# First projections of a hybrid decoder layer: modulation sums queued behind weight low parts, h made two k-tiles at a time, one pace constant changed

## The chip, the cores and the metric

The kernel runs on 1 core of one Trainium2 chip. The metric is the device time of one execution in microseconds (us). Before the change the median of 3 runs is 1785.43 us, from 1785.31 to 1785.56 us.

## The reference, cut to what matters

One decoder layer, 256 tokens of width 2048, float32. The parts that the change touches are the first lines of the reference:

```python
mod = (jax.nn.silu(c) @ w_ada[l] + b_ada[l]).reshape(B, N_MOD, 1, D)
sh1, sc1, gt1, sh2, sc2, gt2 = (mod[:, j] for j in range(N_MOD))
h = rmsnorm(x, g_mix[l]) * (1.0 + sc1) + sh1
z = h @ w_in[l]
```

`silu(c) @ w_ada` is a vector times a 2048 x 12288 matrix. Its first two parts, the shift `sh1` and the scale `sc1`, are needed before `h` exists, and `h` is needed before any product with `w_in` (2048 x 16392). From `z` come three token mixers (an mLSTM, a differential attention and a stick-breaking attention); then follow a projection of each branch, a gated sum, an output projection and a gated MLP. None of these later parts is touched.

## The kernel before, in words

**Precision by splitting.** TensorE multiplies in a rounded float format (fp32r). Each float32 operand is therefore split: ScalarE (ACT) rounds a copy, the high part `hi`; VectorE (DVE) subtracts, the low part `lo = raw - hi`. A product is three matmuls (hi x hi, hi x lo, lo x hi). For weights this is `weights()` (L338 to L355): a DMA of up to four k-tiles (4 x 128 rows by 512 or 440 columns) into a raw tile, then for every two k-tiles one ACT cast (L349) and one DVE subtraction (L351). `state["split"]` always holds the low-part instruction written last.

**The modulation on DVE.** `sh1` and `sc1` aren't computed on TensorE. DVE does multiply-adds over the rows of `w_ada`: `acc += raw[k-tile] * c[k-tile]` with one value of c per partition (`ada_mac`, L225 to L232). TensorE then adds up the 128 partitions with small matmuls against ones (`ada_sums`, L243), DVE adds the bias and the gain (L254 to L256), and `make_h` follows. `ada_first` covers two k-tiles of h at a time (k-tiles 0, 1 and then 2, 3); `ada_quad` covers four (4 to 7, 8 to 11, 12 to 15), with 16 multiply-adds of 128x1024 each. A quad's raw tiles hold two of its 16 rows-of-tiles, 1 MB, loaded by two DMAs of 512 KB (L287).

**make_h** (L465): for every k-tile, ACT applies scale and shift to the normalised, transposed x into a temporary `ht` (L476, from the pool `small`, which has 3 buffers of 256 columns), ACT casts it into the high half of `h1` (L425), and DVE subtracts the low half (L426). k-tiles 0 and 1 go another way (L472 to L474), which the change leaves as it is.

**Rounds.** As h comes in pieces, the 13 column groups of the first projections are worked on in rounds over the k-tiles there are (`visit`, L568, and `partial`, L528): groups 0 to 8 over k-tiles 0 and 1; groups 9 to 12 over 0 to 3; groups 0 to 8 over 2 and 3; groups 0 to 9 over 4 to 7; groups 10 to 12 over 4 to 11; groups 0 to 6 over 8 to 11; then all to the end. Between rounds the partial sums lie in SBUF. Groups 0 to 5 are stick-breaking's queries, keys and values, groups 6 to 12 the two gates of the mLSTM and differential attention's inputs in pieces of 440 columns.

**Pace.** After each column group `tick()` runs (L209). It adds `rates["ada"]` to a counter and lets the modulation's generator make as many steps as the counter holds in whole numbers; a step of `ada_quad` is one multiply-add (and, every second time, the two DMA issues before it). The last argument of `visit` is that rate.

**Order.** The framework's scheduler lays down each engine's instructions at build time. It replays the program with its own estimate of the times; an instruction may go ahead of others on its engine that were written before it, if by that replay it is ready sooner. On the chip every engine then runs its list in that order. `tc.issue_after(x)` forbids the instructions written under it to go ahead of `x` on the same engine. In the kernel before it is used for loads (L286: a modulation load goes behind the last weight load on SyncE, the DMA queue called SP) and for the late modulation's multiply-adds (L302), and not for those of `ada_quad` (L290).

**Buffers.** Weight loads of four k-tiles and modulation loads share four raw tiles of 1 MB (`raw_tile`, L217: three of pool `rawp` and slot `s3`), so a load on SP waits until an earlier raw tile has been read to the end, by an L351 or by an L232, and every load behind it on SP waits too. Weights of two k-tiles (groups 0 to 8 over k-tiles 0, 1 and 2, 3) use another pool (L340).

**`sidewide`** (L73) is a pool of 4 buffers of 512 columns; before the change `make_h` doesn't use it. `late_vectors` (L138) holds two of them while it turns small parameter vectors.

Of the kernel before, what the change touches and what calls it, by code (L numbers as in the profile page):

```python
# [12 lines left out]
AF = mybir.ActivationFunctionType  # L13
# [5 lines left out]
S = 256  # L19
# [20 lines left out]
def kernel(  # L40
# [29 lines left out]
    def wide(name):  # L70
        return tmp.tile([P, 512], F32, tag="wide", name=name, bufs=3)

    def sidewide(name):  # L73
        return tmp.tile([P, 512], F32, tag="sidewide", name=name, bufs=4)

    def small(name):
        return tmp.tile([P, 256], F32, tag="small", name=name, bufs=3)

    V, A, T = nc.vector, nc.scalar, nc.tensor
# [113 lines left out]
    state = {"ada": 0.0, "side": 0.0, "split": None, "load": None, "hold": None, "h": 0, "spare": None}  # L193
# [23 lines left out]
    def raw_tile(nk, n, name):  # L217

        if state["spare"] is not None:
            state["spare"] += 1  # L220
            if state["spare"] % 4 == 0:
                return slots.tile([P, nk, n], F32, tag="s3", name=name)
        return rawp.tile([P, nk, n], F32, tag="raw", name=name)

    def ada_mac(accs, raw, kt0, nk):  # L225
        for k in range(nk):
            kt = kt0 + k
            acc = accs[kt % len(accs)]
            if kt < len(accs):
                V.tensor_scalar(acc, raw[:, k, :], ccol[:, kt:kt + 1], None, ALU.mult)  # L230
            else:
                state["mac"] = V.scalar_tensor_tensor(acc, raw[:, k, :], ccol[:, kt:kt + 1], acc, ALU.mult, ALU.add)  # L232
# [10 lines left out]
    def ada_sums(accs, k0, nk):  # L243

        pm = adaps.tile([P, 512], F32, tag="adaps", name="pm")
        for i, acc in enumerate(accs):
            for k in range(2 * nk):
                m = T.matmul(pm[:, k:k + 1], lhsT=acc[:, k * P:(k + 1) * P], rhs=ones[:, 0:1],  # L248
                             start=k + i == 0, stop=i == len(accs) - 1, skip_group_check=True)
        if k0 == 0:  # L250
            with tc.issue_after(m.ins):
                spin(4)
        ks = slice(k0, k0 + nk)
        V.tensor_tensor(b1[:, ks], pm[:, 0:nk], bsh1_c[:, ks], ALU.add)  # L254
        V.tensor_tensor(a1[:, ks], pm[:, nk:2 * nk], bsc1_c[:, ks], ALU.add)
        V.tensor_tensor(a1[:, ks], a1[:, ks], gmix_c[:, ks], ALU.mult)  # L256
        make_h(k0, k0 + nk)
# [22 lines left out]
    def ada_quad(k0, acc):  # L280

        for q in range(8):
            raw = raw_tile(2, 1024, "raw4")
            for i in range(2):
                r0, c0 = q * 256, i * D + k0 * P
                with tc.issue_after(state["load"].ins):  # L286
                    nc.sync.dma_start(raw[:, :, i * 512:(i + 1) * 512],  # L287
                                      w_ada[r0:r0 + 256, c0:c0 + 512].rearrange("(k p) f -> p k f", p=P))
            for k in range(2):
                ada_mac([acc], raw[:, k:k + 1, :], 2 * q + k, 1)  # L290
                yield
        ada_sums([acc], k0, 4)

# [38 lines left out]
    a1 = const.tile([P, KD], F32, name="a1")  # L332
    b1 = const.tile([P, KD], F32, name="b1")
# [89 lines left out]
    def split(hi, lo, src):  # L423

        A.copy(hi, src)  # L425
        return V.tensor_tensor(lo, src, hi.bitcast(F32), ALU.subtract)  # L426


    h1 = [slots.tile([P, KD // 2, 2 * S], F32R, tag=t, name="h1") for t in ("hh", "hl")]
# [3 lines left out]
    xnT_k = lambda kt: xnT[kt // 8][:, (kt % 8) * S:(kt % 8 + 1) * S]  # L433
# [29 lines left out]
            A.copy(xnT[k2 // 4][:, (k2 % 4) * 512:(k2 % 4 + 1) * 512], pb)  # L463

    def make_h(kt0, kt1):  # L465
        ts = []
        for kt in range(kt0, kt1):
            t = small("ht")
            ts.append(t)
            hi, lo = hact[0](kt), hact[1](kt)  # L470
            if kt0 == 0:
                A.activation(hi, xnT_k(kt), AF.Identity, scale=a1[:, kt:kt + 1], bias=b1[:, kt:kt + 1])  # L472
                V.tensor_scalar(t, xnT_k(kt), a1[:, kt:kt + 1], b1[:, kt:kt + 1], ALU.mult, ALU.add)
                state["split"] = V.tensor_tensor(lo, t, hi.bitcast(F32), ALU.subtract)  # L474
            else:
                A.activation(t, xnT_k(kt), AF.Identity, scale=a1[:, kt:kt + 1], bias=b1[:, kt:kt + 1])  # L476
                state["split"] = split(hi, lo, t)
        if kt0 == 0:
            state["first"] = state["split"]
        state["h"] = kt1  # L480
# [47 lines left out]
    def partial(ci, kt0, kt1):  # L528
        orient, col0, n, dest, scale = first[ci]
        while state["h"] < kt1:  # L530
            pump(ada, 1)
        if kt0 == 0 and ci == 0:
            state["first"], done = state["mac0"], state["first"]
        pin = kt0 == 0 and ci < 2
        if kt0 == 0 and ci < 2:
            kept[ci] = [bank("kept"), bank("kept")]
        acc = kept.get(ci)


        put = acc is None and 0 < kt0 and kt1 < KD and not (kt1 == 4 and ci in (6, 8))  # L540
        if put:
            acc = [gp.tile([P, 512], F32, tag="gp", name="gp") for _ in range(2)]
            for b in range(2):
                for cs, d in dest(b):
                    A.copy(shaped(acc[b][:, cs], d), d)
        acc = gemm(orient, hact, w_in, 0, col0, n, kt0, kt1, hold=state["first"] if pin else None, hold_all=pin,
                   acc=acc)
        if kt0 == 0 and ci == 0:
            state["first"] = done
        for b in range(2):  # L550
            for cs, d in dest(b):
                if ci in kept:
                    if kt1 == KD:
                        A.activation(d, shaped(acc[b][:, cs], d), AF.Copy, scale=scale)
                elif put or kt0 == 0:
                    A.copy(d, shaped(acc[b][:, cs], d))
                else:
                    V.scalar_tensor_tensor(d, shaped(acc[b][:, cs], d), scale, d, ALU.mult, ALU.add)
        tick()
# [3 lines left out]
    quads = slot(4, "quads")  # L563
    ada.append(ada_first(2))
    ada.extend(ada_quad(k0, quads[:, (i % 2) * 1024:(i % 2 + 1) * 1024]) for i, k0 in enumerate((4, 8, 12)))
    done = [0] * 13

    def visit(cis, kt1, rate):  # L568
        rates["ada"] = rate
        for ci in cis:  # L570
            partial(ci, done[ci], kt1)
            done[ci] = kt1

    visit(range(0, 9), 2, 0.62)
    visit(range(9, 13), 4, 1.9)
    visit(range(0, 9), 4, 1.0)
    side.append(late_vectors())
    rates["side"] = 0.4
    visit(range(0, 10), 8, 1.72)
# [343 lines left out]
    for ch in range(2):  # L923
        acc = gemm("T", hact, w_in, 0, C_MO + ch * 512, 512, 0, KD)
# [6 lines left out]
    for ch in range(2):  # L931
        acc = gemm("T", hact, w_in, 0, C_MV + ch * 512, 512, 0, KD)
# [5 lines left out]
    for t, col0, f0 in ((mqT, C_MQ, 0), (mkT, C_MK, 8)):  # L938
        for ch in range(2):
            acc = gemm("H", h1act, w_in, 0, col0 + ch * 512, 512, 0, KD)  # L940
# [44 lines left out]
    for ch in range(4):  # L985
        acc = gemm("T", mact, w_out, 0, ch * 512, 512, 0, KD)
        cs = slice(ch * 512, (ch + 1) * 512)
        for tt in range(NT):
            t = wide("t512")
# [15 lines left out]
        for tt in range(NT):  # L1005
# [5 lines left out]
            with tc.issue_after(m.ins) if last else nullcontext():  # L1011
                for i in range(4):
                    k = 4 * ch + i
                    m = T.transpose(pbs[i // 2][:, (i % 2) * S + tt * P:(i % 2) * S + (tt + 1) * P],
                                    x2[tt][:, k * P:(k + 1) * P], ident)
        for i in range(4):
            k = 4 * ch + i
# [13 lines left out]
    k = 0  # L1031
    while k < KD:
# [4 lines left out]
        for j in range(m):  # L1037
            b = b2[:, k + j:k + j + 1]
            hi, lo = h2act(k + j)[:, 0:S], h2act(k + j)[:, S:2 * S]
# [9 lines left out]
    for half, (c0, c1) in enumerate(((0, 6), (6, NCH))):  # L1049
# [37 lines left out]
        for n in range(4):  # L1087
            acc = gemm("T", act, w_down, c0 * 512, n * 512, 512, 0, 4 * (c1 - c0))
            cs = slice(n * 512, (n + 1) * 512)
            for tt in range(NT):  # L1090
                t = wide("t512")
# [34 lines left out]
```

## Time and profile before

| what | value |
|---|---|
| median of 3 runs | 1785.43 us |
| the profiled execution's own time | 1786.68 us |
| its span on the core | 1785.0 us |
| TensorE busy, matmuls | 1762.3 us, 99% |
| DVE busy | 1302.2 us, 73% |
| ACT busy | 954.2 us, 53% |
| DMA, mean over the span | 237 GB/s |
| first 210 us: DMA share | near 1 in most stretches |

The profile's busy time of TensorE is modelled from pipelined matmuls, so 99% doesn't say that every matmul started as early as it could; what TensorE waited for stands in the view of waits. A line such as "PE gp L403 <- DVE lo L351: 2.3, 1, 2.3" says that matmuls of line 403 into tile gp waited 2.3 us in all, once, for DVE's low part of line 351. The stage that the change touches ends at about 240 us of the span.

### The profile page before, as it was taken

Reading aid. Unit: us, or ns where it says so; the run is one execution under the profiler, and the core shown is the slowest. Engines: PE = TensorE matmul, PEld = TensorE weight load, DVE = VectorE, ACT = ScalarE, POOL = GpSimd, SP = SyncE. Lnnn points to the kernel's source line nnn. Section 1 sums busy time; section 2 is a strip of 40 time slices with the busy share of each in tenths; the row PEclk is TensorE's granted clock in tenths of the full one; section 3 lists DMA queues with packets and bytes.
Section 4 is the critical chain, followed back from the end, with each engine's and each line's share of the span. In section 5 each row is a group of like instructions: output and inputs, shape, how many; then the busy total and the mean of one; then the engine's idle time right before and its main releaser. Section 6 shows DMA issues by size and latency. Waiting matters only on the chain.

```text
span 1785.0 us, 23783 instructions
## 1 busy us (share of the span) xinstructions
PE 1762.3 (99%) x9168; PEld 1514.4 (85%) x9168; DVE 1302.2 (73%) x1734; ACT 954.2 (53%) x1338; POOL 16.7 (1%) x44
## 2 busy tenths in 40 slices
PE   7989999999999999999999999999999999999998
PEld 6889999888778888888888888888888888888887
DVE  6878656888878688777986577888875556666654
ACT  6667555676566566544444555555553345555432
POOL 2000000000000000000000000000000000000000
PEclk9999999999999999999999999999999999999999
DMA  9989755867767667688996557777765555555563
GB/s 330 361 315 336 281 175 166 281 223 250 252 232 260 212 219 252 230 281 285 323 307 212 185 165 247 258 258 268 267 202 201 191 189 189 189 189 189 189 214 116
DMA packets 219730, 423.33 MB, mean 237 GB/s; under 512 B 9026, under 2 KB 31674, under 8 KB 219104
## 3 DMA queue, kind: packets, MB, share of 16 engines
q1 hardware_dynamic: 217328, 417.44, 68.6%
q0 software_dynamic: 1008, 2.23, 0.4%
q10 hardware_dynamic: 1280, 2.14, 0.3%
q8 instruction: 72, 1.18, 0.3%
q14 instruction: 42, 0.34, 0.1%
HBM read 419.68 MB, written 2.10 MB: 236 GB/s over the span
## 4 chain that ended last, share of the span: by engine, by line
PE 96%; DMA 2%; DVE 1%; ACT 0%; issue 0%; SPq 0%; DVEq 0%
PE gp L398 55%; PE acch L384 32%; PE gp L403 2%; PE kept L403 2%; DMA raw<-in_w_ada_dram 1%; PE psc L688 1%; DMA raw<-in_w_in_dram 0%; PE pm L248 0%; DVE quads L232 0%; SPq L271 0%; PE pr L329 0%; DVE lo L351 0%; PE pa L713 0%; PE pm L238 0%; PE pmg L886 0%
## 5 line engine op out<-in xcount | busy, mean ns | idle before, releaser
L351 DVE TENSOR_TENSOR lo<-raw,hi 128x1024 fp32r<-128x1024 f32 (+1 forms) x608 | 724.8, 1208 | 363.0 <-ACT hi L349 325.9
L349 ACT CAST hi<-raw 128x1024 fp32r<-128x1024 f32 (+1 forms) x608 | 619.2, 1039 | 551.0 <-PE gp L398 348.7
L398 PE MATMUL gp<-hi,h 128*128 128x512 f32 (+1 forms) x1600 | 412.5, 386 | 2.1 <-ACT hi L349 1.0
L384 PE MATMUL acch<-h,hi 128*128 128x512 f32 x1664 | 403.6, 391 | 0.2 <-DVE h L1041 0.2
L384 PEld LDWEIGHTS acch<-h,hi 128*128 128x128 f32 x1664 | 303.4, 188 | 58.3 <-DVE h L1041 1.1
L398 PEld LDWEIGHTS gp<-hi,h 128*128 128x128 f32 x1600 | 295.8, 188 | 54.9 <-ACT hi L349 2.8
L398 PE MATMUL gp<-lo,h 128*128 128x512 f32 (+1 forms) x800 | 228.3, 383 | 0.0
L384 PEld LDWEIGHTS acch<-h,lo 128*128 128x128 f32 x1664 | 217.3, 191 | 10.8
L384 PE MATMUL acch<-h,lo 128*128 128x256 f32 x1664 | 220.8, 282 | 0.0
L232 DVE SCALAR_TENSOR_TENSOR acc<-araw,ccol,acc 128x512 f32<-128x512 f32 x240 | 179.0, 746 | 2.8 <-DMA araw<-in_w_ada_dram 1.1
L398 PEld LDWEIGHTS gp<-lo,h 128*128 128x128 f32 x800 | 149.7, 188 | 25.3 <-issue 0.3
L398 PE MATMUL gp<-hi,atl 128*128 128x512 f32 x352 | 137.0, 389 | 0.0
L398 PE MATMUL gp<-hi,ath 128*128 128x512 f32 x352 | 136.9, 389 | 0.0
L398 PE MATMUL gp<-lo,ath 128*128 128x512 f32 x352 | 105.8, 389 | 0.0
L398 PEld LDWEIGHTS gp<-lo,ath 128*128 128x128 f32 x352 | 66.1, 188 | 13.8
L398 PEld LDWEIGHTS gp<-hi,ath 128*128 128x128 f32 x352 | 66.1, 188 | 13.8
L398 PEld LDWEIGHTS gp<-hi,atl 128*128 128x128 f32 x352 | 66.0, 188 | 13.7
L232 DVE SCALAR_TENSOR_TENSOR quads<-raw,ccol,quads 128x1024 f32<-128x1024 f32 x45 | 57.7, 1281 | 11.1 <-DMA raw<-in_w_ada_dram 10.6
L398 PE MATMUL gp<-hi,mgl 128*128 128x512 f32 x128 | 50.3, 393 | 0.0
L398 PE MATMUL gp<-hi,mgh 128*128 128x512 f32 x128 | 50.0, 392 | 0.0
L1066 DVE SCALAR_TENSOR_TENSOR y<-gsum,cols,y 128x255 f32<-128x255 f32 (+1 forms) x88 | 41.4, 478 | 3.3 <-ACT y L1064 2.9
L403 PE MATMUL kept<-h,hi 128*128 128x256 f32 x256 | 39.1, 290 | 2.9 <-ACT h L425 1.1
(365 smaller groups left out, 1605.3 us busy)
## 6 DMA issues: line engine op xcount, KB each, us to landing
raw<-in_w_in_dram SPq DMA_DIRECT2D x98, 1024.0 KB, 5.1
raw<-in_w_up_dram SPq DMA_DIRECT2D x88, 1024.0 KB, 5.1
araw<-in_w_ada_dram SPq DMA_DIRECT2D x128, 512.0 KB, 5.9
raw<-in_w_down_dram SPq DMA_DIRECT2D x44, 1024.0 KB, 5.1
raw<-in_w_ada_dram SPq DMA_DIRECT2D x62, 512.0 KB, 7.4
raw<-in_w_branch_dram SPq DMA_DIRECT2D x24, 1024.0 KB, 6.3
raw<-in_w_in_dram SPq DMA_DIRECT2D x25, 880.0 KB, 5.6
raw<-in_w_out_dram SPq DMA_DIRECT2D x16, 1024.0 KB, 5.0
```

Of the source, the lines that this page charges most:

```text
L232: state["mac"] = V.scalar_tensor_tensor(acc, raw[:, k, :], ccol[:, kt:kt + 1], acc, ALU.mult, ALU.add)
L349: A.copy(hi[:, :, :n], raw[:, k0:k0 + 2, :n])
L351: state["split"] = V.tensor_tensor(lo[:, :, :n], raw[:, k0:k0 + 2, :n], hi[:, :, :n].bitcast(F32), ALU.subtract)
L384: T.matmul(acc[t][:, 0:m], lhsT=w[k // 2][:, k % 2, sl], rhs=ah(s0 + k)[:, 0:m], start=start, stop=s0 + k == kt1 - 1 and w is (wh if flip ...
L398: T.matmul(o, lhsT=a(s0 + k)[:, sl], rhs=wk[:, :n], **kw)
L403: T.matmul(o, lhsT=wk[:, sl], rhs=a(s0 + k), **kw)
L688: T.matmul(pcs[cc][:, o], lhsT=qT[cp, qs], rhs=kT[cp, ks], start=True, stop=True)
L1066: V.scalar_tensor_tensor(yf[:, sft:S], src[:, 0:S - sft], wc(2 - sft), yf[:, sft:S], ALU.mult, ALU.add)
```

## The change

The multiply-adds of `ada_quad` are written under `tc.issue_after(state["split"].ins)`: none of them goes ahead of the low part written last before it on DVE. That is the last L351 of the column group before, or, for the first multiply-add after a `make_h`, that one's low part of h. `make_h` for k-tiles 2 and up goes two k-tiles at a time: two ACT scale-and-shift instructions into the halves of one 512-column temporary, now of the pool `sidewide`, then one cast and one subtraction of 128x512 in place of two of 128x256 each. And the rate of the round of groups 0 to 8 over k-tiles 2 and 3 is 1.15 in place of 1.0.

```diff
             for k in range(2):
-                ada_mac([acc], raw[:, k:k + 1, :], 2 * q + k, 1)
+                with tc.issue_after(state["split"].ins):
+                    ada_mac([acc], raw[:, k:k + 1, :], 2 * q + k, 1)
                 yield
...
     def make_h(kt0, kt1):
-        ts = []
-        for kt in range(kt0, kt1):
-            t = small("ht")
-            ts.append(t)
+        for kt in range(kt0, kt1, 1 if kt0 == 0 else 2):
             hi, lo = hact[0](kt), hact[1](kt)
             if kt0 == 0:
+                t = small("ht")
                 A.activation(hi, xnT_k(kt), AF.Identity, scale=a1[:, kt:kt + 1], bias=b1[:, kt:kt + 1])
...
             else:
-                A.activation(t, xnT_k(kt), AF.Identity, scale=a1[:, kt:kt + 1], bias=b1[:, kt:kt + 1])
-                state["split"] = split(hi, lo, t)
+                t = sidewide("ht")
+                for j in range(2):
+                    A.activation(t[:, j * S:(j + 1) * S], xnT_k(kt + j), AF.Identity, scale=a1[:, kt + j:kt + j + 1],
+                                 bias=b1[:, kt + j:kt + j + 1])
+                both = h1[kt // 8][:, kt % 8:kt % 8 + 2, :]
+                state["split"] = split(both[:, :, 0:S], both[:, :, S:2 * S], t.rearrange("p (k s) -> p k s", k=2))
...
-    visit(range(0, 9), 4, 1.0)
+    visit(range(0, 9), 4, 1.15)
```

## Rows read from the trace of the kernel before

**Rows 1.** Busy time by stretch: start and end in us, then the length and, for each engine, busy us and instructions; at the end TensorE's granted clock, the share of the 16 DMA engines and GB/s.

```profile
26.00:76.00 50.00, 47.95 (x272) 43.62 (x273) 42.69 (x57) 31.02 (x53) 0.00 (x0) 0.97 1.03 357
76.00:104.00 28.00, 27.12 (x180) 24.61 (x179) 22.43 (x28) 18.82 (x33) 0.00 (x0) 1.00 0.90 328
104.00:130.00 26.00, 21.67 (x169) 20.93 (x168) 22.12 (x25) 14.23 (x21) 0.00 (x0) 1.00 0.89 311
130.00:210.00 80.00, 80.00 (x465) 74.89 (x464) 61.91 (x62) 53.26 (x93) 0.00 (x0) 1.00 0.95 339
...
330.00:1050.00 720.00, 719.48 (x3434) 595.31 (x3433) 566.67 (x810) 399.34 (x569) 4.99 (x10) 1.00 0.72 245
1050.00:1785.00 735.00, 729.92 (x3872) 630.55 (x3871) 497.45 (x626) 347.14 (x456) 1.95 (x4) 1.00 0.62 209
...
70.00:80.00 10.00, 10.00 (x62) 9.58 (x61) 7.76 (x7) 7.47 (x12) 0.00 (x0) 1.00 1.04 388
```

**Rows 2.** What TensorE waited for from 26 to 230 us: us in total, times, longest.

```profile
PE gp L403 <- DVE lo L351: 2.3, 1, 2.3
PE kept L403 <- ACT h L425: 1.1, 1, 1.1
PE gp L398 <- ACT hi L349: 1.0, 3, 0.7
PE kept L403 <- ACT hi L349: 1.0, 1, 1.0
PE kept L403 <- ACT h L472: 0.8, 1, 0.8
PE gp L398 <- ACT h L425: 0.5, 1, 0.5
PE gp L398 <- DVE h L426: 0.4, 1, 0.4
PE gp L398 <- DVE dq L558: 0.2, 1, 0.2
```

**Rows 3.** TensorE in order of time, 117 to 126 us: start, us, line, tiles, shape, count, and the idle time before with what ended it.

```profile
120.03 1.24 PE L403 MATMUL gp<-h,hi 128*128 128x256 f32 x9
123.56 0.50 PE L403 MATMUL gp<-h,lo 128*128 128x256 f32 x2 [2.29 <-DVE lo L351]
```

**Rows 4.** DVE in order of time, 112 to 127 us, in the same form.

```profile
113.35 2.60 DVE L232 SCALAR_TENSOR_TENSOR quads<-raw,ccol,quads 128x1024 f32<-128x1024 f32 x2
119.76 2.60 DVE L232 SCALAR_TENSOR_TENSOR quads<-raw,ccol,quads 128x1024 f32<-128x1024 f32 x2 [3.81 <-DMA raw<-in_w_ada_dram]
122.28 3.49 DVE L351 TENSOR_TENSOR lo<-raw,hi 128x1024 fp32r<-128x1024 f32 x3
```

**Rows 5.** ACT in order of time, 99 to 111 us.

```profile
100.80 1.59 ACT L476 ACTIVATE ht<-xnT,b,a 128x256 f32<-128x256 f32 x3 [0.62 <-DVE a L256]
...
103.39 1.02 ACT L425 CAST h<-ht 128x256 fp32r<-128x256 f32 x3
104.31 2.01 ACT L349 CAST hi<-raw 128x1024 fp32r<-128x1024 f32 x2
106.21 0.62 ACT L476 ACTIVATE ht<-xnT,b,a 128x256 f32<-128x256 f32 x1
...
108.16 0.42 ACT L425 CAST h<-ht 128x256 fp32r<-128x256 f32 x1
...
108.99 2.02 ACT L349 CAST hi<-raw 128x1024 fp32r<-128x1024 f32 x2
```

**Rows 6.** The chain that ended last, 95 to 101 us: start, us, what.

```profile
97.55 1.69 PE pm L248 x16
...
99.49 0.71 DVE quads L232
```

**Rows 7.** Issues on SP in order of time, 43 to 66 us and 100 to 130 us.

```profile
53.85 0.88 SPq L287 DMA_DIRECT2D raw<-in_w_ada_dram  x2
57.77 0.37 SPq L344 DMA_DIRECT2D raw<-in_w_in_dram  x1
...
109.66 0.37 SPq L344 DMA_DIRECT2D raw<-in_w_in_dram  x1
```

**Rows 8.** Single loads, asked for by the moment of their issue: of those issued at 50.88, 90.81 and 109.66 us, the size and the us from issue to landing.

```profile
raw<-in_w_in_dram SPq DMA_DIRECT2D x1, 880.0 KB, 8.3
...
raw<-in_w_in_dram SPq DMA_DIRECT2D x1, 440.0 KB, 4.4
...
raw<-in_w_in_dram SPq DMA_DIRECT2D x1, 1024.0 KB, 4.9
```

**Rows 9.** Groups of equal shape on DVE and ACT, 0 to 240 us: count, busy us, mean ns of one, idle before. The second is ACT's copy of the same width as the new pair.

```profile
L426 DVE TENSOR_TENSOR h<-ht,h 128x256 fp32r<-128x256 f32 x14 | 5.5, 419 | 2.5 <-ACT h L425 2.5
...
L545 ACT COPY gp<-skT 128x512 f32<-128x512 f32 x12 | 7.1, 596 | 0.2
```

**Rows 10.** In order of time: DVE from 50 to 61 us, ACT from 55 to 60 us, and of DVE from 289 to 290 us a subtraction of 128x512 of another part.

```profile
57.66 1.28 DVE L232 SCALAR_TENSOR_TENSOR quads<-raw,ccol,quads 128x1024 f32<-128x1024 f32 x1
58.86 0.75 DVE L426 TENSOR_TENSOR h<-ht,h 128x256 fp32r<-128x256 f32 x2
...
57.82 0.73 ACT L425 CAST h<-ht 128x256 fp32r<-128x256 f32 x2
...
289.52 0.68 DVE L426 TENSOR_TENSOR loA<-spA,hiA 128x512 fp32r<-128x512 f32 x1
```

## The prediction, written before the result was known

> **What bounds the kernel now.** I read the stretches first [rows 1]. From 1050 us TensorE is busy 729.92 of 735 us, from 330 to 1050 us 719.48 of 720: nothing the change touches lies there, so what is won or lost in the first projections reaches the end one for one, as long as TensorE stays the last engine. The stage of the change is 26 to 230 us. There the DMA engines are nearly full too: share 1.03 from 26 to 76 us, 0.90, 0.89 and 0.95 after. Between 104 and 130 us TensorE is busy for only 21.67 of 26 us, and the loads run at 311 GB/s where one stretch shows 388: neither is full. Something between them holds both up. The clock is 1.00 from 76 us on; the waits that may go aren't tied to a lower clock, and I count nothing for it.
>
> Then the waits [rows 2]: they sum to 7.3 us. This is the ceiling: less the 0.8 us for the first h (L472, not touched), at most 6.5 us of 1785 can be had in this stage by taking waits away.
>
> The three largest lie together. At 120 us TensorE has done nine hi matmuls of a group, then idles 2.29 us for a low part [rows 3]. On DVE [rows 4] that low part (122.28) stands behind two multiply-adds that start at 119.76, and these idled 3.81 us for their DMA. The cast it needs isn't late: DVE moves on to low parts without a gap. At 107 us [rows 5] the h of the fourth k-tile is late: three scale-and-shifts run at 100.80, the fourth only at 106.21, since `ht` has three buffers; its cast ends at 108.58, TensorE waits 1.1 us for it, and the next weight cast, pushed back on ACT to 108.99, costs 1.0 us more [rows 2].
>
> **Part 1, multiply-adds behind low parts.** Removes nothing, adds nothing: 48 multiply-adds change place. Around 120 us, counting ticks at 1.72 a group, the two at 119.76 and the second of the pair at 113.35 were written with or after the group whose low parts start at 122.28. The second of the 113.35 pair and the first of the 119.76 pair were written behind that group's low parts and the last behind the next group's, so all three drop behind. The low parts then start once cast. TensorE's 2.3 us go. Next late there could be the group's load: below.
>
> Price: a multiply-add that runs later frees its raw tile later, and SP issues the next load into it later. The worst place is 52 to 61 us. The first multiply-add of the first quad ran in a gap before h; it now waits for h's low part. That one stands at 58.86, behind a multiply-add of 1.28 us [rows 10]; behind one cast of 0.60 us that starts at 57.82 [rows 9, 10] it moves up to some 58.45. With the pair (0.68 us, [rows 10]) it ends near 59.1, then 0.75 us for the first multiply-add and 1.28 us for the second give 61.2 in place of 53.8. The modulation load issued at 53.85 [rows 7] slips by 7.4 us. Does the DMA run dry? The load issued at 50.88 lands 8.3 us later, at 59.2; the next weight load, issued at 57.77 [rows 7], can't land in less than a lone load takes: 440 KB took 4.4 us [rows 8], of which 1.16 us are bytes at 388 GB/s [rows 1], so 3.2 us are fixed. Its bytes start near 61.0: a gap of at most 1.9 us. But this weight load then no longer queues behind 1 MB of modulation (2.7 us at 388 GB/s), so weights land sooner and only the modulation falls back. Bounds -1.0 to +1.9 us; I take +0.3, nearer to nothing, since the quad's own sums are placed at 97.55 [rows 6], some 9 us after its last load can have landed (two issued by 79 us).
>
> The trace's 3.2 us of fixed time stand against the Trainium skill, "DMA: Bandwidth & Descriptors", section "Anatomy of one DMA", which fits about 2.0 us per DMA on the GpSimd path. By that figure the gap would be an estimated 0.6 us and the term 0.1, and the time 0.2 us lower. No run of before shows a lone load that fast.
>
> The load issued at 109.66 [rows 7] waited for a low part that stood behind a 1.28 us multiply-add; alone it took 4.9 us [rows 8], to 114.6. It is the group's that TensorE begins at 120.03 [rows 3], at 117.9 once the 2.1 us of part 2 are gone. Even unmoved it lands 3 us ahead of that, and one cast and one low part take 1.0 and 1.2 us: bounds 0 to +0.5, I take 0.
>
> **Part 2, h in pairs.** Per pair two casts of 0.41 us (0.31 apart in the rows at 103.39) become one of 0.60 (the copy of that width, 0.596) [rows 5, 9]; two subtractions of 0.419 [rows 9] become one of 0.68 [rows 10]. Over 7 pairs ACT and DVE save about 0.2 us a pair each, beside TensorE's work: nothing directly. What counts is that four buffers of two k-tiles don't stop at the third k-tile: four scale-and-shifts from 100.80, two casts, all four high parts by about 104 in place of 108.58. The 1.1 us and the 1.0 us behind it go: -2.1. Even if `late_vectors` still holds two of the four buffers, the two others hold four k-tiles. Cost: the first k-tile waits for its partner. At 57.8 us the first high part comes 0.2 us later, the low parts 0.5 us earlier, with waits of 0.5 and 0.4 us there [rows 2]: bounds -0.9 to +0.4, I take 0.
>
> **Part 3, the rate 1.15.** Nine groups make 10 steps in place of 9, so every later modulation step is written one group earlier or at the same place, the sums of k-tiles 4 to 7 one group (2.4 to 2.7 us) earlier. A multiply-add that stood inside the bias chain at 99.49 for 0.71 us [rows 6] also can't stand there now: it waits for h. TensorE would reach the sums near 95.2, the last multiply-add ends at about 95.3: bounds -0.6 (the remaining waits for hi) to +0.3; I take 0, as the wait it serves is already counted.
>
> **Sum.** -2.3 (low part) -2.1 (fourth h) +0.3 (DMA gap) = -4.1 us; the other terms 0. Loads must keep up with a TensorE that is 4 us ahead: from 104 to 210 us 311 x 26 + 339 x 80 = 35.2 MB move, which at 388 GB/s is 91 us of 106. They can. Against the profiled execution: 1786.68 - 4.1 = 1782.6 (span 1785.0, 1.7 outside). The timed median, 1785.43, lies 1.25 below that execution, so the forecast is 1781.3 us.
>
> **Rivals.**
> *More than that.* The waits at 57 us (0.9) and two of the three hi waits (0.7) go too and the gap doesn't form: another 2 us, 1779.4. For it: DVE has no multiply-add before a low part any more. Against: those casts wait on ACT's list or on landings, which aren't touched.
> *Given back to the loads.* Waits go, but the next load is late each time: 1.9 us at 59 and 0.5 at 115 us by the bounds above, and 0.5 once more after 130 us, 2.9 us on -4.4: 1783.9. For it: share 0.95 after 130 us. Against: the sum of bytes above.
> *Slower: SP blocked in order.* One mechanism: SP issues in a fixed order; if the scheduler leaves a modulation load ahead of a weight load while the multiply-add that frees its tile has moved back, the weight load waits. At 57.77 that is 61.2 + 0.88 = 62.1, 4.3 us late; less the 1 us or so by which casts lead TensorE, 3.4 us of TensorE, there and at the second quad's start, while the 2.3 us come back in this form: -2.1 + 6.8 = +4.7, 1790.1. It decides as soon as one such pair keeps its order on SP. For it: 53.85 does come before 57.77 now. Against: the same replay that places multiply-adds places loads and knows of the new constraint.
> *It does nothing.* The multiply-adds would have been placed so anyway: 1785.4. Against: rows 4 show the overtaking.
>
> **How the numbers follow.** A change under 0.2% (3.6 us) can't be told from none. Forecast 0.46 (own range 1780.0 to 1783.0, from nothing to twice the DMA term and 1 us for later work laid down anew; the better part lies under 1781.9: faster 0.32, same 0.14); more 0.16 (faster); given back 0.17 (same); blocked 0.17 (slower); nothing 0.04 (same). Faster 0.48, same 0.35, slower 0.17. The range leaves out the lower tail of "more" and the dearer half of "blocked": 1777.5 to 1789.0.
>
> **What would show it.** Right: no wait of TensorE for L351 in the group whose cast stands near 115 us; DVE idle before L232 may stay, with nothing behind it; all four h of k-tiles 4 to 7 cast before 105 us; no "kept" wait for L425; low parts of h of 128x512 at about 0.68 us; from 130 us on the same matmuls about 4 us earlier, up to the end. Wrong: a TensorE wait for a weight cast that itself waited for its DMA, near 60 or 115 us; SP waiting for L232 ahead of an L344; or matmuls early at 130 us and the lead gone by 330 us.

## The result, and the profile after

The change makes the kernel slower by 0.24%: 1789.84 us against 1785.43 us, medians of 11 runs each, ratio 1.0024 with a 95% interval of 1.0014 to 1.0033. The forecast was 1781.3 us with a range of 1777.5 to 1789.0: the sign is wrong and the time lies outside.

| what | before | after |
|---|---|---|
| median | 1785.43 us | 1789.84 us |
| profiled execution, its span | 1786.68, 1785.0 us | 1789.25, 1787.5 us |
| third quad's first multiply-add starts | 151.85 us | 160.94 us |
| longest wait of TensorE, 150 to 185 us | none | 2.9 us |

The two profiled executions are 2.57 us apart, the medians 4.41: the one of before lies 1.25 us above its median, the one of after 0.59 below. The traces can explain 2.57 us of it; for the rest go by the experiments and their intervals.

First the same stretches as [rows 1], of after: start and end, length, busy us of TensorE, its weight loads, DVE, ACT and GpSimd, then TensorE's clock, DMA share and GB/s. The last three rows cut 20 us out of the fourth, and 2 us out of these.

```profile
26.00:76.00 50.00, 48.39 (x281) 44.54 (x280) 40.88 (x49) 28.76 (x51) 6.21 (x13) 0.97 0.99 338
76.00:104.00 28.00, 26.40 (x165) 23.30 (x164) 22.25 (x27) 19.71 (x32) 0.00 (x0) 1.00 1.02 372
104.00:130.00 26.00, 24.50 (x190) 23.24 (x189) 23.32 (x28) 15.70 (x21) 0.00 (x0) 1.00 0.84 297
130.00:210.00 80.00, 77.13 (x426) 71.46 (x425) 59.47 (x58) 49.86 (x88) 0.00 (x0) 0.98 0.90 319
160.00:170.00 10.00, 9.43 (x48) 8.50 (x46) 9.14 (x10) 5.34 (x13) 0.00 (x0) 1.00 0.60 204
170.00:180.00 10.00, 7.70 (x31) 7.12 (x32) 6.69 (x7) 4.95 (x10) 0.00 (x0) 0.83 1.03 375
...
162.00:164.00 2.00, 2.00 (x12) 1.88 (x11) 2.00 (x3) 2.00 (x6) 0.00 (x0) 1.00 0.00 0
```

From 104 to 130 us TensorE won what was meant to be won: 24.50 us busy in place of 21.67. The loss is new, and it is in the stretch that had none, 130 to 210 us: 77.13 in place of 80.00. It sits in 20 us of it. The DMA engines are only 0.60 busy from 160 to 170 us (0.92 before), and from 162 to 164 us they move nothing at all. In the next 10 us TensorE's clock is 0.83.

Now TensorE's waits from 26 to 230 us, for [rows 2]; three of 0.4 us are left out.

```profile
PE gp L399 <- ACT hi L350: 4.1, 3, 2.9
PE kept L404 <- DVE lo L352: 0.9, 1, 0.9
PE kept L404 <- ACT hi L350: 0.6, 1, 0.6
PE gp L399 <- DVE lo L352: 0.6, 1, 0.6
...
```

Lines of code are one higher than before (L351 is now L352, L425 L426, L403 L404). The 2.3 us for a low part and the 1.1 us for an h are gone. The sum is 7.4 us, no less than the 7.3 of before, because one wait of 2.9 us for a weight cast has come in. Without it, waits fell by 2.8 us.

How the lead turns into a loss shows on TensorE at two places of equal work: the first 512-column matmuls of the round over k-tiles 4 to 7, and the same 440-column group near 232 us (564 matmuls lie between the two in either kernel). First before, then after.

```profile
134.09 2.00 PE L398 MATMUL gp<-hi,h 128*128 128x512 f32 x8
...
231.08 1.76 PE L398 MATMUL gp<-hi,h 128*128 128x440 f32 x8
```

```profile
132.06 2.00 PE L399 MATMUL gp<-hi,h 128*128 128x512 f32 x8
...
168.46 0.96 PE L399 MATMUL gp<-lo,h 128*128 128x440 f32 x4
172.30 5.02 PE L399 MATMUL gp<-hi,h 128*128 128x440 f32 x16 [2.87 <-ACT hi L350]
177.15 1.76 PE L399 MATMUL gp<-lo,h 128*128 128x440 f32 x8
...
233.69 1.76 PE L399 MATMUL gp<-hi,h 128*128 128x440 f32 x8
```

The lead is 2.03 us at 132 us, and 2.61 us behind at 232: 4.64 us are lost between, and the 2.61 stay to the end (the spans are 2.5 apart). The rows show the place. TensorE stands for 2.87 us, and the 16 matmuls after it take 5.02 us. Eight of them take 1.76 elsewhere, one every 0.20 us, so 16 would take 3.36: another 1.66 us, in the stretch whose clock is 0.83. 2.87 + 1.66 = 4.53.

Who came late? The same 20 us on DVE, SP and ACT of after, in order of time (L287 issues a modulation load, L345 a weight load).

```profile
153.11 2.06 DVE L352 TENSOR_TENSOR lo<-raw,hi 128x880 fp32r<-128x880 f32 x2 [3.47 <-ACT hi L350]
...
159.73 1.29 DVE L427 TENSOR_TENSOR h<-ht,h 128x512 fp32r<-128x512 f32 x2
160.94 0.75 DVE L230 TENSOR_SCALAR quads<-raw,ccol 128x1024 f32<-128x1024 f32 x1
161.72 1.28 DVE L232 SCALAR_TENSOR_TENSOR quads<-raw,ccol,quads 128x1024 f32<-128x1024 f32 x1
162.92 2.05 DVE L352 TENSOR_TENSOR lo<-raw,hi 128x880 fp32r<-128x880 f32 x2
164.89 2.60 DVE L232 SCALAR_TENSOR_TENSOR quads<-raw,ccol,quads 128x1024 f32<-128x1024 f32 x2
```

```profile
143.99 0.88 SPq L287 DMA_DIRECT2D raw<-in_w_ada_dram  x2
...
149.67 0.88 SPq L287 DMA_DIRECT2D raw<-in_w_ada_dram  x2
155.20 0.37 SPq L345 DMA_DIRECT2D raw<-in_w_in_dram  x1
163.03 0.88 SPq L287 DMA_DIRECT2D raw<-in_w_ada_dram  x2
165.00 0.37 SPq L345 DMA_DIRECT2D raw<-in_w_in_dram  x1
```

```profile
171.32 1.75 ACT L350 CAST hi<-raw 128x880 fp32r<-128x880 f32 x2 [5.49 <-DMA raw<-in_w_in_dram]
```

The cast that TensorE lacks waits 5.49 us for a weight load that SP issued at 165.00 (6.2 us to its landing). Before 165.00 SP issued one weight load at 155.20 and then nothing until 163.03. What had changed is L230, the first multiply-add of the third quad (k-tiles 12 to 15): it now stands right behind the low parts of h of k-tiles 8 to 11. Before, the same instruction ran at 151.85 us:

```profile
151.85 0.75 DVE L230 TENSOR_SCALAR quads<-raw,ccol 128x1024 f32<-128x1024 f32 x1
```

Its data had been asked for at 144 us in both kernels.

### The profile page after: what moved, and what is told of

The parts are those of the page before. It is cut to its first block, busy times and chain, and to the rows that moved or that the text cites. A ratio compares the mean times of both kernels' runs of the same rounds, so it can differ in the third digit from the quotient of the medians.

```text
span 1787.5 us, 23735 instructions
## 1 busy us (share of the span) xinstructions
PE 1764.6 (99%) x9168; PEld 1515.9 (85%) x9168; DVE 1302.6 (73%) x1727; ACT 952.2 (53%) x1331; POOL 16.4 (1%) x44
## 4 chain that ended last, share of the span: by engine, by line
PE 95%; DMA 2%; DVE 1%; ACT 1%; issue 0%; SPq 0%; DVEq 0%; ACTq 0%
PE gp L399 53%; PE acch L385 32%; PE kept L404 3%; PE gp L404 3%; DMA raw<-in_w_in_dram 1%; ACT hi L350 1%; DMA raw<-in_w_ada_dram 1%; PE psc L691 1%; DVE lo L352 0%; ACT ht L477 0%; DVE quads L232 0%; PE pr L330 0%; PE pa L716 0%; PE pm L238 0%; PE pmg L889 0%
## 5 line engine op out<-in xcount | busy, mean ns | idle before, releaser
L352 DVE TENSOR_TENSOR lo<-raw,hi 128x1024 fp32r<-128x1024 f32 (+1 forms) x608 | 724.2, 1208 | 357.4 <-ACT hi L350 323.3
L350 ACT CAST hi<-raw 128x1024 fp32r<-128x1024 f32 (+1 forms) x608 | 617.8, 1039 | 557.5 <-PE gp L399 340.6
L399 PE MATMUL gp<-hi,h 128*128 128x512 f32 (+1 forms) x1600 | 412.8, 387 | 4.7 <-ACT hi L350 4.1
L399 PEld LDWEIGHTS gp<-hi,h 128*128 128x128 f32 x1600 | 297.1, 189 | 57.8 <-ACT hi L350 6.2
L399 PE MATMUL gp<-lo,h 128*128 128x512 f32 (+1 forms) x800 | 228.1, 383 | 0.6 <-DVE lo L352 0.6
L232 DVE SCALAR_TENSOR_TENSOR acc<-araw,ccol,acc 128x512 f32<-128x512 f32 x240 | 179.0, 746 | 4.2 <-DMA araw<-in_w_ada_dram 2.4
L399 PEld LDWEIGHTS gp<-lo,h 128*128 128x128 f32 x800 | 149.6, 188 | 26.5 <-DVE lo L352 1.2
L399 PE MATMUL gp<-hi,atl 128*128 128x512 f32 x352 | 136.9, 389 | 0.0
L399 PE MATMUL gp<-hi,ath 128*128 128x512 f32 x352 | 136.8, 389 | 0.0
L399 PE MATMUL gp<-lo,ath 128*128 128x512 f32 x352 | 105.8, 389 | 0.0
L399 PEld LDWEIGHTS gp<-lo,ath 128*128 128x128 f32 x352 | 66.1, 188 | 13.8
L399 PEld LDWEIGHTS gp<-hi,ath 128*128 128x128 f32 x352 | 66.1, 188 | 13.7
L399 PEld LDWEIGHTS gp<-hi,atl 128*128 128x128 f32 x352 | 66.1, 188 | 13.7
L232 DVE SCALAR_TENSOR_TENSOR quads<-raw,ccol,quads 128x1024 f32<-128x1024 f32 x45 | 57.7, 1282 | 3.8 <-DMA raw<-in_w_ada_dram 3.1
L399 PE MATMUL gp<-hi,mgl 128*128 128x512 f32 x128 | 50.3, 393 | 0.0
L399 PE MATMUL gp<-hi,mgh 128*128 128x512 f32 x128 | 50.0, 392 | 0.0
L404 PE MATMUL kept<-h,hi 128*128 128x256 f32 x256 | 39.0, 291 | 1.0 <-ACT hi L350 0.6
```

The source lines that it names most:

```text
L350: A.copy(hi[:, :, :n], raw[:, k0:k0 + 2, :n])
L352: state["split"] = V.tensor_tensor(lo[:, :, :n], raw[:, k0:k0 + 2, :n], hi[:, :, :n].bitcast(F32), ALU.subtract)
L399: T.matmul(o, lhsT=a(s0 + k)[:, sl], rhs=wk[:, :n], **kw)
L404: T.matmul(o, lhsT=wk[:, sl], rhs=a(s0 + k), **kw)
```

## The experiments

**Theory.** For the third quad's first multiply-add the low part "written last" is that of h. The quad's first two loads (issued at 143.99 and 149.67 us) lie in two of the four raw tiles and may not be read until that h is done. The weights have too few tiles left, and TensorE starves. It is the order alone, at this one place. **Rivals:** the pairs or the rate make the loss; it is spread over all quads; SP is merely blocked in order, a weight load standing behind a modulation load that may not start (the prediction's own rival); or DVE's order itself delays the weights' low parts.

### The parts one by one, and a weaker order

e1 keeps pairs and rate, and puts the quads' multiply-adds behind the last low part of *weights* only:

```diff
-                with tc.issue_after(state["split"].ins):
+                with tc.issue_after(state["wlow"].ins):
...
                                                  ALU.subtract)
+            state["wlow"] = state["split"]
```

> The whole change, but the multiply-adds of a quad go behind the last low part of weights, never behind those of h; so the first two of the third quad may run before h is made. Theory (the first multiply-adds of the third quad behind h's low parts hold a raw tile, SP issues nothing from 155.2 to 163.0 us, a weight load lands at 171.2 and TensorE waits 2.9 us, then runs some matmuls at the lower clock): the wait for a weight cast near 169 us is under 0.5 us and the time is about 4.5 us below the changed kernel, 1785.3 (1783.5 to 1786.5). Rival (the pairs or the rate make the loss): the time stays at 1788.5 to 1791.

e2 is the kernel before with the new order alone, e3 with the pairs alone, e4 with the rate of 1.15 alone.

> Only the multiply-adds behind low parts; h one k-tile at a time, rate 1.0. Theory: the first multiply-adds of the third quad wait for h here too, so a wait for a weight cast of 2 us or more after the third piece of h, 1787 to 1791 although the 2.3 us wait of before is gone. Rivals (pairs, rate): no such wait, 1782.5 to 1785.

> Only h in pairs; multiply-adds free, rate 1.0. Theory: the wait for the fourth k-tile's h and the cast behind it go (2.1 us), the wait of 2.3 us for a low part stays: 1783.3 (1782 to 1785.5). Rival (the pairs make the loss): 1788 or more.

> Only the rate 1.15. Theory: 1785.4 within 1.5 us, since nothing is held longer. Rival (the rate brings the third piece of h into the start of the round of groups 10 to 12 and starves its loads): 1788 or more with a wait for a weight cast near 165 to 175 us.

Measured, as ratios to the kernel before on the same chip (1785.98 us there; e5 to e8 and e9 to e11 ran on two other chips, each beside the kernel before): e1 0.9985 (0.9976 to 0.9993), e2 1.0032 (1.0019 to 1.0044), e3 0.9989 (0.9980 to 0.9998), e4 0.9994 (0.9986 to 1.0003). The order alone is slower than the whole change, either of the other parts is a little faster or the same, and an order that lets go of h is faster than before. DVE and SP of e2 in order of time:

```profile
168.76 0.42 DVE L427 TENSOR_TENSOR h<-ht,h 128x256 fp32r<-128x256 f32 x1
169.10 0.75 DVE L230 TENSOR_SCALAR quads<-raw,ccol 128x1024 f32<-128x1024 f32 x1
169.88 5.25 DVE L232 SCALAR_TENSOR_TENSOR quads<-raw,ccol,quads 128x1024 f32<-128x1024 f32 x4
```

```profile
173.83 0.37 SPq L345 DMA_DIRECT2D raw<-in_w_in_dram  x1
```

And what SP waited for from 163 to 174.2 us:

```profile
SPq L345 <- DVE quads L232: 10.1, 1, 10.1
```

Here the picture is plainer than in the change itself. Without the pairs the fourth h comes last, L230 runs at 169.10, the weight load waits 10.1 us for a multiply-add to free its tile, and TensorE waits 3.9 us.

Two more put single parts back. e7 undoes the order and keeps pairs and rate; e10 undoes the rate (1.15 to 1.0) and keeps order and pairs.

> The change without its first part: h in pairs and the rate of 1.15 stay, multiply-adds stand where the scheduler likes. Theory: no wait above 2.5 us, no stretch of 10 us at a clock under 0.95 between 100 and 230 us; each part alone gave 0.999 of the time before, so both 1783 to 1785.5. Rival (the parts hurt each other, whatever the order of the multiply-adds): above 1787.5.

> Order and pairs, with the rate of that round back at 1.0. Theory (the order alone makes the loss, the rate has no part in it): L230 of the third quad behind the low parts of h, a wait for L350 of 2 us or more between 160 and 185 us, 1787 to 1792. Rival (the rate brings the third quad's loads too early and so fills the tiles): 1783 to 1786.

e7: ratio 0.9980 (0.9971 to 0.9988), 1782.86 us where the kernel before took 1786.70, the lowest ratio of all and faster than both kernels of this case. Between 150 and 185 us TensorE waits for nothing. e10: 1.0026 (1.0016 to 1.0036), L230 at 166.66 us, a wait of 4.9 us. The rival of pairs and rate falls on both sides.

### Which quad

e5 frees the third quad alone, e6 holds it alone (the name `wlow` as in e1):

```diff
-                with tc.issue_after(state["split"].ins):
+                with tc.issue_after(state["wlow" if k0 == 12 else "split"].ins):
```

> The change, but the third quad (k-tiles 12 to 15) alone may go behind the low part of weights written last; it no longer waits for the low parts of h. The first two quads stay as in the change. Theory (two of the four raw tiles lie full of modulation that may not be read before h of k-tiles 8 to 11 is done, so the weights have too few tiles left): L230 of the third quad runs before 156 us in place of 160.94, the longest idle time on SP between 140 and 185 us is under 5 us in place of 7.1, and the wait of 2.9 us for L350 and the stretch at a clock of 0.83 go; 4.5 us less than the change: about 1785.3, 1784 to 1786.5. Rival (the loss is spread over all quads, the third is only where it shows): above 1788.

> The other way round: the first two quads go behind low parts of weights alone, the third behind the low part written last, as in the change. Theory: the third quad is enough for the loss; TensorE waits 2 to 4 us for one L350 that itself waited for its load, between 160 and 185 us, the clock falls below 0.9 in one stretch of 10 us behind it, and the time is 1787 to 1791. Rival (spread over all quads): 1784.5 to 1786.5, about a third of the loss.

Against 1786.70 us for the kernel before on that chip, e5 took 1786.48, ratio 1.0000 (0.9991 to 1.0009), and e6 1791.67, 1.0026 (1.0016 to 1.0035). The loss against before moves with the third quad: freeing it takes the loss away, and holding it alone is enough. Of e6, TensorE in order of time (L400 is L399 of the change), then the stretch:

```profile
171.76 5.02 PE L400 MATMUL gp<-hi,h 128*128 128x440 f32 x16 [2.62 <-ACT hi L350]
```

```profile
170.00:180.00 10.00, 7.09 (x26) 6.22 (x27) 4.77 (x5) 3.68 (x6) 0.00 (x0) 0.83 1.05 380
```

It is the wait of the change again (2.62 us), followed by the same 5.02 us. In e5 the wait for L350 is gone, but one of 1.8 us for an ACT copy into `gp` stands in its place, which is why e5 only comes back to the time of before. Why e1 (0.9985) and e7 (0.9980) do better than e5 beyond that wait is open: with the third quad free, holding the first two may cost something of its own. Beside the third's hold it doesn't show (the change 1.0024, e6 1.0026).

### Tiles, SP's order, or DVE's order

e8 leaves DVE's order as in the change and takes the third quad's loads out of the four raw tiles, into three buffers of 512 KB, issued by GpSimd:

```diff
-            raw = raw_tile(2, 1024, "raw4")
+            own = k0 == 12
+            raws = [adap.tile([P, 2, 512], F32, tag="ada", name="raw5") for k in range(2)] if own else None
+            raw = None if own else raw_tile(2, 1024, "raw4")
...
+                    if own:
+                        r1 = q * 256 + i * P
+                        nc.gpsimd.dma_start(raws[i], w_ada[r1:r1 + P, :].rearrange("p (j f) -> p j f", f=D)
+                                          [:, 0:2, k0 * P:k0 * P + 512])
```

> The change with its order as it is (the third quad's multiply-adds behind the low part of h), but that quad's loads go one k-tile at a time (512 KB, both halves in one transfer) into the three buffers of 512 KB that the late modulation uses later, and are issued on GpSimd's queue. So the four raw tiles and SP belong to the weights. Theory (held tiles, by way of transfers): L230 of the third quad still stands behind the low parts of h at about 160 us, yet no weight cast waits over 1.5 us of TensorE between 150 and 185 us; 1782 to 1786. Rival (the order on DVE itself, multiply-adds bunched behind h that push the low parts of weights back): TensorE waits for L352 in place of L350, 2 us or more, and the time stays above 1787.5.

e9 leaves them in the raw tiles and changes the queue only:

```diff
-                    nc.sync.dma_start(raw[:, :, i * 512:(i + 1) * 512],
+                    (nc.gpsimd if k0 == 12 else nc.sync).dma_start(raw[:, :, i * 512:(i + 1) * 512],
```

> The change, with the third quad's loads still in the shared raw tiles, but issued on GpSimd's queue; DVE's order stays within one instruction of the change's around 160 us. Theory (held tiles): the first two loads of the third quad still hold two of the four raw tiles from about 150 us until L230 and L232 read them at 161 to 167 us; the load that TensorE lacks gets its tile when a low part of weights ends near 165 us, as in the change, so most of the wait for L350 stays: 1786 to 1790. Rival (SP blocked in order: a load that could start stands behind one that may not): SP is free, the weight load goes at about 158 us, and the time is 1782 to 1785.

e8: 0.9987 (0.9978 to 0.9996). e9: 1.0025 (1.0015 to 1.0035). This pair decides between the three, with one thing left over: e8 also loads in other pieces (both halves of one k-tile in one transfer), which wasn't tried apart. DVE around 160 us, of e8 and then of e9:

```profile
160.99 0.75 DVE L230 TENSOR_SCALAR quads<-raw,ccol 128x1024 f32<-128x1024 f32 x1
161.78 1.28 DVE L232 SCALAR_TENSOR_TENSOR quads<-raw,ccol,quads 128x1024 f32<-128x1024 f32 x1
```

```profile
160.90 0.75 DVE L230 TENSOR_SCALAR quads<-raw,ccol 128x1024 f32<-128x1024 f32 x1
161.68 1.29 DVE L232 SCALAR_TENSOR_TENSOR quads<-raw,ccol,quads 128x1024 f32<-128x1024 f32 x1
```

They agree to 0.1 us, the low part of weights behind them too (162.98 and 162.89), yet from 150 to 185 us e8's TensorE waits for nothing and e9's waits 4.2 us. So it isn't DVE's order as such. And in e9 the third quad's loads are off SP, so no weight load stands behind them. SP's waits of e9 between 155.5 and 165.2 us, then its issues, then one of GpSimd's:

```profile
SPq L345 <- DMA raw<-in_w_in_dram: 5.2, 1, 5.2
SPq L345 <- DVE lo L352: 4.5, 1, 4.5
```

```profile
154.95 0.37 SPq L345 DMA_DIRECT2D raw<-in_w_in_dram  x1
...
164.97 0.37 SPq L345 DMA_DIRECT2D raw<-in_w_in_dram  x1
```

```profile
158.34 1.44 POOL L287 DMA_DIRECT2D raw<-in_w_ada_dram  x2 [7.57 <-DVE lo L352]
```

With SP free the weight load goes at 164.97, in the change at 165.00. It waits for its own tile: for the weight load before it to land (5.2 us) and for that one's low parts to be read (4.5 us). Back in the change, 155.20 is the end of the low parts of 153.11 (155.17) and 165.00 that of the low parts of 162.92 (164.97). So from 155.20 to 165.00 us one raw tile takes all new weight loads, at one load in 10 us. Two of the others hold modulation until 163.00 and 167.49, the ends of L232. The fourth, freed by a low part at 158 us, goes to the next modulation load, as GpSimd's row of e9 shows. SP's 7 idle us in the change are real but stand beside the cause. DVE's order has a share by way of the tile: the cast of the load of 155.20 starts at 161.12, its first half of two is done near 162.0 (an estimate from the cast's 1.77 us), and the low part behind L232 starts at 162.92, so the tile comes free some 0.9 us later than it could. In e8, with the same order on DVE, no weight load hangs on that.

e11 takes both gains together: e7 with e8's buffers and no order.

> Pairs, the rate of 1.15, no order, and the third quad's loads in the 512 KB buffers on GpSimd's queue. No theory needs it; it asks whether what e7 and e8 gain adds up. If more raw tiles for the weights still help where nothing is held: 1780 to 1782.5. If e7 has no wait left that a raw tile could take away: as e7, 1782 to 1784.5.

It is the slowest of all, 1.0045 (1.0032 to 1.0059). Its stretches from 110 us, then one of e8:

```profile
110.00:130.00 20.00, 19.59 (x163) 19.16 (x162) 16.77 (x20) 9.71 (x13) 2.29 (x4) 1.00 1.04 386
130.00:160.00 30.00, 24.00 (x117) 20.51 (x116) 26.39 (x28) 19.64 (x36) 4.93 (x7) 0.94 1.03 373
```

```profile
130.00:160.00 30.00, 30.00 (x159) 26.65 (x158) 22.47 (x24) 25.07 (x47) 0.00 (x0) 1.00 0.90 317
```

With nothing to hold it, the third quad begins at 110.61 us, and its modulation is loaded among the weights. The DMA engines are full (1.04, 1.03), TensorE is busy for 24.00 of 30 us and waits 4.9 us for two weight casts. In e8 three such loads lie in their buffers and the fourth is issued at 162.04. That these early loads take the weights' share fits the rows; it wasn't tried apart.

Third quad's first multiply-add, longest wait of TensorE from 150 to 185 us, and ratio:

| kernel | third quad's L230 at | wait | ratio |
|---|---|---|---|
| before | 151.85 us | none | 1 |
| e1, e3, e4, e5, e7 | 148.0 to 150.8 us | up to 0.8; e5 1.8 (ACT copy) | 0.9980 to 1.0000 |
| change, e2, e6, e9, e10 | 160.3 to 169.1 us | 2.6 to 4.9 us | 1.0024 to 1.0032 |
| e8, own buffers | 160.99 us | none | 0.9987 |

Against the ranges written beforehand, e1 (1783.38 us) and e7 (1782.86) came out below, e2 (1791.69), e6 (1791.67) and e9 (1790.84) above, each by less than 1 us. e3's wait of 2.3 us for a low part of weights, said to stay, was gone, and e11 fits neither of its two.

## Why the prediction was wrong, point by point

**The failed step is the price of part 1**, "The worst place is 52 to 61 us". I read the start of the first quad [rows 10], found its multiply-add behind a low part of h, bounded the slip, and took it for the worst. The first quad's L230 does run behind h now, at 57.80 us, and there is no loss: TensorE is busy for 48.39 us from 26 to 76 where it was 47.95, at a DMA share of 0.99. The +0.3 us was harmless, and not by the way it was worked out: the load that was to slip from 53.85 to 61.2 us went at 56.80, after a wait for a low part of weights and not for a multiply-add. (The gap of 1.9 us there is 1.8 by its own terms, 61.0 less 59.2; nothing hangs on it.) The same sentence applied to the third quad, whose first multiply-add ran at 151.85 before any h there, was never worked out. There the hold is 9.1 us (151.85 to 160.94) for loads asked for at 144 us, and what it costs is tiles to load weights into: TensorE idles 2.87 us for a weight cast and loses 1.66 us behind it.

**"Loads must keep up … They can"** summed bytes against 388 GB/s. It holds on the average and missed the point: from 160 to 170 us the DMA engines were 0.60 busy. They had bandwidth; what was short was a tile to load into.

**The rival "SP blocked in order"** gave 1790.1 us, and 1789.84 was measured, but that is luck: it was right by its sign and nearly its size, not by its mechanism. It was placed at 57.77 us and the second quad's start, where nothing was lost, and e9 shows that taking the block away on SP changes nothing. The chance of 0.17 for slower came from an argument on issue order; one on tiles held would have had a row of before for it.

**"The waits that may go aren't tied to a lower clock, and I count nothing for it"** was true of the waits that went. The one that came was followed by a clock of 0.83 and 1.66 us more, over a third of the loss.

**Part 1, -2.3 us.** The wait at 122 us went as foretold, but the order isn't needed for it: with pairs alone (e3) or rate alone (e4) the 2.3 us are gone too, and e1 with a weaker order is no faster than e7 without any. Each of these edits lays the rows near 120 us down anew. Nor does DVE have "no multiply-add before a low part any more", as a rival put it. Around 109 us in the change:

```profile
106.93 1.21 DVE L352 TENSOR_TENSOR lo<-raw,hi 128x1024 fp32r<-128x1024 f32 x1
108.07 1.28 DVE L232 SCALAR_TENSOR_TENSOR quads<-raw,ccol,quads 128x1024 f32<-128x1024 f32 x1
109.26 1.22 DVE L352 TENSOR_TENSOR lo<-raw,hi 128x1024 fp32r<-128x1024 f32 x1
```

A multiply-add written earlier still goes between two low parts, and TensorE waits 0.9 us for the second. The constraint keeps an instruction from overtaking an older low part; it doesn't clear the way for a newer one.

**Part 2, -2.1 us.** On ACT it went as foretold. All four h of k-tiles 4 to 7 are scaled from 98.77 us on and cast by 103.2, and a low part of 128x512 takes 0.69 us (0.68 foretold):

```profile
98.77 2.08 ACT L477 ACTIVATE ht<-xnT,b,a 128x256 f32<-128x256 f32 x4 [1.75 <-DVE a L256]
102.03 1.14 ACT L426 CAST h<-ht 128x512 fp32r<-128x512 f32 x2
```

The 1.1 us went, of the 1.0 us behind it 0.6 stay. The pairs by themselves, e3, measure 0.9989, -2.0 us of 1786 (-3.6 to -0.4), but the agreement with -2.1 is luck. In e3 (lines numbered as before) the second low part of h stands behind low parts of weights and a multiply-add on DVE, and TensorE waits for it at the same place:

```profile
109.08 1.01 PE L403 MATMUL kept<-h,hi 128*128 128x256 f32 x3 [2.44 <-DVE h L426]
```

This is more than the 2.1 us that the pairs take away there. TensorE's waits from 26 to 230 us still sum to less in e3 than before (6.1 and 7.3 us), but the 2.3 us at 122 us are among what is gone. The term counted when h is cast, and not when its low part is done.

**Parts 1 and 2 together** were to put TensorE 4.4 us ahead by 130 us; it was 2.03 ahead. The waits fell by 2.8 us, as 0.6 us of part 2 stayed and waits of 0.9 and 0.6 us for low parts came in. So the lead that I counted on was twice what was there, even before it was lost.

**Part 3** was costed at nothing, and e4 (0.9994, 0.9986 to 1.0003) and e10 agree. The remark in it that a multiply-add "can't stand there now: it waits for h" was the loss itself, seen at the second quad and counted as a gain.

Two of the three signs named beforehand held up. "A TensorE wait for a weight cast that itself waited for its DMA" came (at 172 us, not 60 or 115), and "matmuls early at 130 us and the lead gone by 330" came by 180. The third, SP waiting for L232 ahead of a weight load, tells nothing by itself: from 26 to 230 us it stands nine times in either kernel, only longer in the change (9.4 us at most, 3.3 before).

## What to carry to other kernels

Before an instruction that reads a shared buffer is tied behind another, list every place where the tie applies and see what comes just before each: a tie to "the last one written" means weights in one place and a late h in another. In this case the price of waiting had to be counted in buffers held and the time they are held, not in the DMA's bytes; DMA engines that idle while the consumer of their loads starves were the mark of it. A wait that one edit removes by reshuffling the rows around it isn't that edit's merit until another edit has been seen to leave it there.

## What the chip showed that I had not expected

**Matmuls after a stall.** After 2.87 us of idle time 16 matmuls took 5.02 us in place of 3.36, at a granted clock of 0.83 over the 10 us (between the levels of 1.2 and 2.4 GHz, so partly at the lower). In e9 4.2 us of idle time were followed by 16 in 5.67 us and a stretch at 0.66. In e10 4.95 us were followed by 8 in 3.18 us in place of 1.76, with 0.89 and then 0.94 over two such stretches; so what is lost behind a stall (1.66, 2.31 and 1.42 us) didn't grow with its length. The idle 2.29 us of before [rows 3] left its stretch at 1.00 [rows 1], and the 1.8 us of e5 left 1.00.

**A load into idle DMA engines.** In e2 SP had issued nothing for 10 us, and from 172 to 174.8 us the DMA engines moved nothing. This is the weight load issued at 173.83 us:

```profile
raw<-in_w_in_dram SPq DMA_DIRECT2D x1, 880.0 KB, 4.4
```

880 KB at 388 GB/s [rows 1] are 2.3 us, which leaves about 2.1 us, an estimate. The prediction took 3.2 us from the 440 KB load of [rows 8], which took as long with half the bytes. That one met idle engines too (nothing moved from 89.8 to 91.7 us), and behind both SP issued 1 MB of modulation, 0.42 and 0.46 us later. So the two rows don't give one fixed time, and why the smaller load took as long is open. The figure of some 2.0 us in the Trainium skill, "DMA: Bandwidth & Descriptors", section "Anatomy of one DMA", stated there for the GpSimd path, agrees with the 2.1 us better than the row I preferred to it.
